# Twelve weight tiles of a hybrid decoder layer: low parts by an accumulating DMA in place of a VectorE subtract

## The chip, the core and the metric

The kernel runs on one core of a Trainium2 chip. The time is that of one execution on the device, in microseconds (us). Of several runs the median is given, with the lowest and the highest. Beside the runs, one execution was recorded by the profiler; its trace tells when each instruction ran on each engine. The engines are named as in the profile: PE (TensorE, matmuls), DVE (VectorE), ACT (ScalarE), POOL (GpSimd) and SP (SyncE, here only an issuer of DMAs).

## What is computed

One layer of a decoder trunk over 16 meta tokens and 1024 tokens of width 1024, in float32. Cut to what matters here:

```python
z = h @ w_in + b_in                       # 1024 -> 512 q, 128 k, 128 v, 2 x 512 conv, 2 x 1024 gates
a = swa_sink_attention(q, k, v, sinks, rel_bias)
c = c_val * jax.nn.sigmoid(c_gate)
c = jax.nn.silu(layer_norm(causal_dwconv(c, conv_dw, conv_dw_b), conv_ln_g, conv_ln_b))   # 31 taps
mixed = sigmoid(g_attn) * (a @ w_attn_proj) + sigmoid(g_conv) * (c @ w_conv_proj)
h = layer_norm(ALPHA * h + mixed @ w_out, ln1_g, ln1_b)
f = (gelu(g) * u) @ ffn_w_down            # u, g = split(causal_dwconv(h @ ffn_w_up)), 3 taps
h = layer_norm(ALPHA * h + f, ln2_g, ln2_b)
```

## The kernel before

**Precision by split operands.** Every float32 operand of a matmul is held as two float32r tiles: a high part (the value rounded to float32r) and a low part (value minus high part). A product is three matmuls, low x high, high x high, high x low, into the same PSUM bank (`product`, L336 to L345). So each weight tile passes through a split before TensorE may use it: `split` (L299 to L303) lets ScalarE copy the raw float32 tile into the high part (L300) and VectorE subtract the high part from the raw tile into the low part (L303).

**Weight tiles.** `weights` (L318 to L334) delivers a tile of 128 x 1024 (all 1024 rows of the weight, 128 output columns, as eight blocks of 128 columns). It takes a raw buffer from the pool `wraw` (tag `wr`, two buffers), has SP load it (`fill`), takes a pair of high and low parts from the pool `wsp` (tag `w`, two buffers) and splits. It counts its calls; below, tile n is the n-th call. Tiles 1 to 30 are those of `w_z`, the in-projection (L357 to L359: a tile's output for four groups of some 260 columns, 96 matmuls and 11 us on TensorE where nothing else stands between). Tiles 1 to 14 are k, v, q, most of the conv input and gates 0 and 1; tiles 15 to 17 gates 2 to 4, tiles 18 and 19 the last conv chunk, tiles 20 to 30 gates 5 to 15. Tiles 31 to 38 are those of `w_ab` (the loop over m at L1162), whose 128 output columns of the attention projection and of the conv projection are formed together and merged with the gates; there a product takes high x high, high x low, low x high (L1157 to L1172), so that the low part of the weight is read by the third matmul.

With two buffers of `w`, the copy of tile n waits until TensorE has read the last of tile n-2, which is the moment at which it begins tile n-1; so each tile is split while TensorE works on the tile ahead. With two buffers of `wr`, SP loads the raw tile n+2 as soon as the split of tile n has read its own.

**What stands beside.** From 171 to about 326 us TensorE alternates tiles 15 to 24 with banded attention (scores L919 and L920, transposes L943), while VectorE runs the depthwise conv, 31 taps for each of four chunks (L747, L749), GpSimd adds the chunks up once the third is done (`csum`, L972 and L973) and the rest of the LayerNorm over the conv follows up to about 385 us (mean by ones matmuls L982 and L984, squares L1030 and L1033, variance, roots L1045, silu L1057, splits L1063 and L1064). Gate outputs leave PSUM by a ScalarE tanh (L758) and are stored to a scratch `sgd` in DRAM by a DMA that ScalarE issues (L129). From 412 to about 500 us follow the eight tiles of `w_ab`. Per tile and group VectorE multiplies the gates by the two PSUM results (L1183, L1184), adds (L1185), and ScalarE and VectorE split the result (L1192, L1193). The gates come back from `sgd` by SP, four loads to a tile, into five slots of `OB`. The matmul results of the first branch lie in three PSUM buffers of tag `mm`, which the in-projection uses too, those of the second in two of tag `t`.

**What sets the order.** The program is written against a scheduler that simulates the engines and orders the instructions of each engine by rank (`with rank(...)`) and readiness. A split has rank 500, an evacuation 600, which come ahead of nearly all else that is ready. The order of each engine is thus fixed when the program is built, and each engine runs its list in order.

## Time and profile before

| | us |
|---|---|
| median of 3 runs | 1255.88 (1255.16 to 1256.59) |
| span of the profiled execution | 1253.2 |
| TensorE busy in it | 1239.1 |
| VectorE busy | 1078.1 |
| ScalarE busy | 627.4 |
| GpSimd busy | 7.4 |

For the profiled execution the span is the time that is known; the runs' median is 2.7 us longer. Busy time leaves out the issuing of DMAs and waits. A row of a timeline gives start, duration, engine, line, operation, out<-in, shape, and in brackets the idle time ahead of it with what ended it. A row of the waits gives the waiting engine and line, what it waited for, and the total, the number and the longest in us. The mean granted clock of TensorE was 0.999 of its full rate.

### The profile page before, as it was taken

What the parts mean: (1) busy time and instruction counts of PE and PEld (TensorE: products, weight loads), DVE (VectorE), ACT (ScalarE), POOL (GpSimd) and SP (SyncE); (2) the same over time, 40 slices, a digit from 0 to 9 for tenths busy, and PEclk for the clock granted to TensorE, in tenths of its full rate; (3) what the DMA queues carried; (4) which work ended last, traced back from release to release, by engine and by line L of the source; (5) the groups of instructions that cost most, each with busy time, mean ns of one, the idle gap of its engine ahead of it and who ended that gap; (6) DMA issues with size and microseconds to landing.
All of it is one profiled execution on the core that took longest, in us unless ns stands there. A gap on an engine that the chain in (4) does not pass through costs nothing.

```text
span 1253.2 us, 23194 instructions
## 1 busy us (share of the span) xinstructions
PE 1239.1 (99%) x9176; PEld 1173.8 (94%) x9176; DVE 1078.1 (86%) x1862; ACT 627.4 (50%) x1284; POOL 7.4 (1%) x8
## 2 busy tenths in 40 slices
PE   8999999999999999999999999999999999999997
PEld 7999999999999999788899999999999998888886
DVE  8989999999978677448899999998999977896697
ACT  8533255655474233344676556565565654545330
POOL 0000000001000000000000000000000000000000
PEclk9999999999999999999999999999999999999999
DMA  7383633432256564222145555453454567998712
GB/s 261 117 292 102 191 93 98 109 95 81 73 157 173 170 164 119 85 94 75 68 160 191 194 197 201 161 211 137 163 206 175 196 227 251 395 342 330 276 60 84
DMA packets 98687, 212.20 MB, mean 169 GB/s; under 512 B 11395, under 2 KB 38595, under 8 KB 98322
## 3 DMA queue, kind: packets, MB, share of 16 engines
q1 hardware_dynamic: 84414, 199.57, 46.9%
q10 hardware_dynamic: 14164, 11.15, 2.8%
q8 instruction: 72, 1.18, 0.4%
q14 instruction: 37, 0.30, 0.1%
HBM read 150.29 MB, written 62.70 MB: 170 GB/s over the span
## 4 chain that ended last, share of the span: by engine, by line
PE 96%; DVE 2%; ACT 1%; DMA 1%; issue 0%; SPq 0%; DVEq 0%; ACTq 0%
PE px L1594 15%; PE py L1594 10%; PE ps_x L1739 9%; PE ps_z L340 8%; PE ps_z L343 8%; PE ps_z L344 8%; PE ps_z L1739 7%; PE ps_p L1172 7%; PE pz L1594 5%; PE pw L1594 5%; PE ps_w L344 2%; PE ps_w L343 2%; PE ps_w L340 2%; PE ps_z L575 2%; PE ps_t L943 1%; PE ps_s L919 1%
## 5 line engine op out<-in xcount | busy, mean ns | idle before, releaser
L340 PE MATMUL ps_z<-RHO,w 128*128 128x256 f32 (+2 forms) x864 | 243.2, 281 | 0.0
L343 PE MATMUL ps_z<-RHO,w 128*128 128x256 f32 (+2 forms) x864 | 242.3, 280 | 0.0
L344 PE MATMUL ps_z<-RHC,w 128*128 128x256 f32 (+2 forms) x864 | 242.2, 280 | 0.0
L343 PEld LDWEIGHTS ps_z<-RHO,w 128*128 128x128 f32 x864 | 162.5, 188 | 0.5
L344 PEld LDWEIGHTS ps_z<-RHC,w 128*128 128x128 f32 x864 | 162.7, 188 | 0.2
L340 PEld LDWEIGHTS ps_z<-RHO,w 128*128 128x128 f32 x864 | 162.5, 188 | 0.1
L749 DVE SCALAR_TENSOR_TENSOR FA<-cin,cdw,FA 128x1026 f32<-128x1026 f32 x120 | 154.3, 1295 | 0.7
L300 ACT CAST w<-wr 128x1024 fp32r<-128x1024 f32 x37 | 38.8, 1048 | 64.0 <-PE ps_z L344 48.0
L1412 DVE TENSOR_TENSOR RHO<-wr,RHO 128x512 fp32r<-128x512 f32 x94 | 64.0, 684 | 3.6 <-ACT RHO L1411 3.5
L1411 ACT CAST RHO<-wr 128x512 fp32r<-128x512 f32 x94 | 56.9, 619 | 15.6 <-DVE wr L1429 7.9
L1429 DVE TENSOR_TENSOR wr<-wr 128x512 f32<-128x512 f32 x88 | 60.1, 683 | 0.1
L758 ACT ACTIVATE FA<-ps_z,colr 128x258 f32<-128x258 f32 (+1 forms) x64 | 30.1, 472 | 59.0 <-PE ps_z L344 50.7
L303 DVE TENSOR_TENSOR w<-wr,w 128x1024 fp32r<-128x1024 f32 x37 | 45.1, 1218 | 7.6 <-ACT w L300 7.4
L1606 ACT COPY FA<-px 128x516 f32<-128x516 f32 (+2 forms) x23 | 13.1, 571 | 71.2 <-PE px L1594 71.2
L1172 PE MATMUL ps_p<-OC,w 128*128 128x256 f32 (+1 forms) x384 | 48.1, 278 | 0.0
L1172 PE MATMUL ps_p<-OA,w 128*128 128x256 f32 (+1 forms) x384 | 47.8, 278 | 0.0
L1172 PEld LDWEIGHTS ps_p<-OC,w 128*128 128x128 f32 x384 | 46.2, 188 | 0.1
L1172 PEld LDWEIGHTS ps_p<-OA,w 128*128 128x128 f32 x384 | 45.9, 188 | 0.0
L1412 DVE TENSOR_TENSOR w<-wr,w 128x512 fp32r<-128x512 f32 x60 | 40.7, 684 | 4.7 <-ACT w L1411 4.7
L1594 PE MATMUL px<-OA,RHO 128*128 128x260 f32 x324 | 43.0, 282 | 0.0
L1594 PE MATMUL px<-OC,RHO 128*128 128x256 f32 x324 | 41.2, 276 | 0.8 <-DVE OB L1345 0.8
L1594 PE MATMUL px<-RHC,RHO 128*128 128x256 f32 (+1 forms) x312 | 40.6, 279 | 0.1
(457 smaller groups left out, 3109.3 us busy)
## 6 DMA issues: line engine op xcount, KB each, us to landing
wr<-in_w_up_dram SPq DMA_DIRECT2D x44, 512.0 KB, 3.6
wr<-in_w_z_dram SPq DMA_DIRECT2D x29, 512.0 KB, 4.2
OB<-in_w_down_dram SPq DMA_DIRECT2D x24, 512.0 KB, 5.2
fd<-FA SPq DMA_DIRECT2D x44, 256.0 KB, 2.0
FA<-sd SPq DMA_DIRECT2D x15, 512.0 KB, 8.9
qt<-qd SPq DMA_DIRECT2D x28, 256.0 KB, 4.1
OB<-td SPq DMA_DIRECT2D x14, 512.0 KB, 8.7
sgd<-FA ACTq DMA_DIRECT2D x48, 128.0 KB, 2.4
```

The costliest lines, as they stand in the source:

```text
L300: ins = nc.scalar.copy(hi, raw)
L303: return nc.vector.tensor_tensor(lo, raw, f32(hi), OP.subtract)
L340: ins = nc.tensor.matmul(ps, al, bh, start=i == 0, stop=False)
L343: nc.tensor.matmul(ps, ah, bh, start=False, stop=False)
L344: last = nc.tensor.matmul(ps, ah, bl, start=False, stop=i == n - 1)
L749: nc.vector.scalar_tensor_tensor(acc[c], cin[:, j:j + U], wc, acc[c], OP.mult, OP.add)
L1172: nc.tensor.matmul(ps[:, :b - a], x, rhs(k, hl, a, b), start=k + j == 0, stop=k == 3 and j == 2)
L1411: nc.scalar.copy(hi, src)
L1412: ins = nc.vector.tensor_tensor(lo, src, f32(hi), OP.subtract)
L1429: ins = nc.vector.tensor_tensor(*x)
L1594: ins = nc.tensor.matmul(o, (ah, ah, al)[j][:, k * P:(k + 1) * P], bmat(sub, q, j, k), start=first and i == 0, stop=i == 11, skip_group_ch ...
L1739: nc.tensor.matmul(banks[i], l[:, ts], r[:, ws], start=first and a and x + k == 0, stop=z and x == len(ops) - 1 and k == 2, skip_group_che ...
```

## The change

Odd tiles above 14, twelve in all (15, 17, 19, 21, 23, 25, 27 and 29 of the in-projection, 31, 33, 35 and 37 of `w_ab`), get their low part in another way. ScalarE copies the high part as before and then writes the negative of the high part into the low part's place. Two DMAs issued by GpSimd, one for the partitions 0 to 63 and one for 64 to 127, then add the raw tile to what stands there. VectorE's subtract of these tiles is gone. The raw buffer comes free when the DMAs have landed. [...]

```diff
-    colr = constr.tile([P, n_right], F, name="colr")
+    colr = constr.tile([P, n_right + 8], F, name="colr")[:, :n_right]
...
         hi, lo = chunks(sp.tile([P, W_LEN], R, name="w3") if own else wsp())
         if n <= 3:
             return hi, lo, raw
+        if n > 14 and n % 2:
+            with rank(RK_SPLIT):
+                nc.scalar.copy(hi, raw)
+                nc.scalar.mul(lo, f32(hi), -1.0)
+                for p in (0, 64):
+                    nc.gpsimd.dma_start(out=f32(lo)[p:p + 64], in_=raw[p:p + 64], accum_op=OP.add)
+            return hi, lo
         with rank(RK_SPLIT):
             last_split.append(split(raw, hi, lo))
...
-    OC = late.tile([P, 8376], R, name="OC")
+    OC = late.tile([P, 8320], R, name="OC")
...
-    nc = _bacc.Bacc("TRN2", target_bir_lowering=False, num_devices=1, dynamic_dma_scratch_size=64)
+    nc = _bacc.Bacc("TRN2", target_bir_lowering=False, num_devices=1, dynamic_dma_scratch_size=256)
```

The lines behind the new branch stand 7 further on in the changed kernel (L758 is L765 there, L1192 is L1199). The copy of a changed tile is L330, the multiplication L331, the DMAs L333.

ScalarE's list at the copy of tile 35, which is made while tile 34 is on TensorE (`RHO`, `RHC` and `pair` are splits of the merged result, `RX` a split of an output weight). Before:

```order
L1192 ACTIVATE RHO<-OB 128x2x128
L300 CAST w<-wr 128x1024
L1192 ACTIVATE RHC<-OB 128x2x128
L300 CAST RX<-FA 128x1024
L1187 ACTIVATE pair<-OB 128x2
```

The same place after:

```order
L1199 ACTIVATE RHO<-OB 128x2x128
L330 CAST w<-wr 128x1024
L1199 ACTIVATE RHC<-OB 128x2x128
L300 CAST RX<-FA 128x1024
L331 ACTIVATE w<-w 128x1024
L1194 ACTIVATE pair<-OB 128x2
```

The multiplication stands two instructions behind its copy, with another full-sized CAST between; in most of the twelve places it is one short instruction.

SP's list at the raw tiles 37 and 38 and the first of two output weights that use the same buffers (`wr<-in_w_ab_dram` is a raw tile, `OB<-sgd` the gates of one group, 258 columns for the first group of a tile). Before:

```order
L125 DMA FA<-in_w_out_dram 128x1024
L125 DMA wr<-in_w_ab_dram 128x1024
L125 DMA OB<-sgd 128x2x258
L125 DMA OB<-sgd 128x2x256 x3
L125 DMA wr<-in_w_ab_dram 128x1024
L125 DMA OB<-sgd 128x2x258
L125 DMA OB<-sgd 128x2x256 x3
L125 DMA wr<-in_w_out_dram 128x1024
L125 DMA OB<-sgd 128x2x258
L125 DMA OB<-sgd 128x2x256 x3
```

The same place after:

```order
L125 DMA FA<-in_w_out_dram 128x1024
L125 DMA OB<-sgd 128x2x258
L125 DMA OB<-sgd 128x2x256
L125 DMA wr<-in_w_ab_dram 128x1024
L125 DMA OB<-sgd 128x2x256 x2
L125 DMA wr<-in_w_ab_dram 128x1024
L125 DMA OB<-sgd 128x2x258
L125 DMA OB<-sgd 128x2x256 x3
L125 DMA OB<-sgd 128x2x258
L125 DMA wr<-in_w_out_dram 128x1024
L125 DMA OB<-sgd 128x2x256 x3
```

The load that waits for the DMAs of tile 35 now stands between the gate loads of a tile, two ahead of it and two behind; the one that waits for those of tile 37 has one gate load ahead and three behind.

On GpSimd the eight DMAs of tiles 15, 17, 19 and 21 stand ahead of the two additions for `csum`, the sixteen others behind them. TensorE's list is the same up to about 170 us and from the first `w_ab` tile on; between, attention's matmuls stand somewhat earlier among those of the tiles, and the mean's matmuls of the LayerNorm stand 18 matmuls earlier. VectorE's list loses the 12 subtracts and is otherwise reordered in the attention stage.

## Prediction

> **What bounds the kernel now.** I read first the busy times of the page, then the chain that ended last, then the waits of TensorE, then the three stretches in which the twelve changed tiles are prepared.

> From the page of the profile, the busy times and the chain by engine:

> ```profile
> PE 1239.1 (99%) x9176; PEld 1173.8 (94%) x9176; DVE 1078.1 (86%) x1862; ACT 627.4 (50%) x1284; POOL 7.4 (1%) x8
> PE 96%; DVE 2%; ACT 1%; DMA 1%; issue 0%; SPq 0%; DVEq 0%; ACTq 0%
> ```

> From the view of waits, TensorE's own (in total, times, longest, in us):

> ```profile
> PE ps_w L590 <- DVE ones L239: 1.7, 1, 1.7
> PE ps_h L518 <- DVE xn L497: 1.5, 1, 1.5
> PE pw L1594 <- ACT FA L1392: 1.2, 1, 1.2
> PE px L1594 <- DVE OB L1345: 0.8, 1, 0.8
> PE ps_z L572 <- ACT FA L524: 0.3, 1, 0.3
> PE ps_s L919 <- DVE sm L923: 0.3, 1, 0.3
> ```

> From the view of windows, the in-projection tiles beside conv and attention, the last of them beside the conv LayerNorm, and the two-branch projection:

> ```profile
> core 0: us, PE busy (x) PEld busy (x) DVE busy (x) ACT busy (x) POOL busy (x), PEclk, DMA share, GB/s
> 171.00:326.00 155.00, 154.69 (x1259) 151.40 (x1257) 151.36 (x324) 85.49 (x227) 5.30 (x2) 1.00 0.34 95
> 326.00:413.00 87.00, 87.00 (x740) 86.50 (x739) 72.64 (x133) 46.34 (x79) 0.00 (x0) 1.00 0.54 152
> 413.00:480.00 67.00, 67.00 (x583) 67.00 (x582) 47.38 (x110) 18.77 (x40) 0.00 (x0) 1.00 0.54 151
> ```

> The reader is to see that TensorE does the chain by itself (96%), waits six times in the whole program, and in the three stretches is busy for 154.69 + 87.00 + 67.00 = 308.69 of 309.00 us at a granted clock of 1.00. VectorE is busy for 151.36 of 155 us in the first stretch, close behind, but TensorE waits for it there once, for 0.3 us. So in the changed stretch a shorter queue on VectorE can give back at most 0.3 us, as long as a matmul takes the time that it takes now.

> **The change, part by part.** The split of a tile has two rows in the page's costliest groups:

> ```profile
> L300 ACT CAST w<-wr 128x1024 fp32r<-128x1024 f32 x37 | 38.8, 1048 | 64.0 <-PE ps_z L344 48.0
> L303 DVE TENSOR_TENSOR w<-wr,w 128x1024 fp32r<-128x1024 f32 x37 | 45.1, 1218 | 7.6 <-ACT w L300 7.4
> ```

> Removed: 12 subtracts of 1.218 us = 14.6 us of VectorE. It has no row in TensorE's waits but the 0.3 us, so this is worth 0 to 0.3 us; I take 0.

> Added on ScalarE: 12 multiplications of a 128x1024 tile. The row nearest is the CAST of the same shape on the same engine, so 12 x 1.05 = 12.6 us. ScalarE is busy for 85.49 of 155, 46.34 of 87 and 18.77 of 67 us: it has room. What is queued behind a multiplication are evacuations of PSUM, each later by up to 1.05 us; three buffers of the tag `mm` cover that except where ScalarE is full, between 356 and 385 us (a rival, below). I take 0.

> Added on GpSimd: 24 DMAs of 256 KB, two to a tile. GpSimd has two instructions in these stretches. Eight of the DMAs (tiles 15 to 21) stand ahead of them and sixteen behind, and those sixteen thus wait as well for what the first of the two waits for, the third chunk's taps. In the timeline these two, and the copies of tiles 23 to 26 on ScalarE:

> ```profile
> 282.13 2.43 POOL L972 TENSOR_TENSOR csum<-FA 128x1026 f32<-128x1026 f32 x1 [279.46 <-DVE FA L749]
> 284.63 2.87 POOL L973 TENSOR_TENSOR csum<-csum,FA 128x1026 f32<-128x1026 f32 x1
> ```

> ```profile
> 300.61 1.03 ACT L300 CAST w<-wr 128x1024 fp32r<-128x1024 f32 x1
> 316.48 1.05 ACT L300 CAST w<-wr 128x1024 fp32r<-128x1024 f32 x1 [1.12 <-PE ps_z L344]
> 331.10 1.05 ACT L300 CAST w<-wr 128x1024 fp32r<-128x1024 f32 x1 [1.94 <-PE ps_z L344]
> 343.66 1.05 ACT L300 CAST w<-wr 128x1024 fp32r<-128x1024 f32 x1 [2.24 <-PE ps_z L344]
> ```

> csum ends at 287.5, and tile 23, the first behind it, is copied at 300.61: 13 us to spare, so 0.

> Now the term that decides: **the new path of a low part**. Before, copy and subtract follow each other. Now copy, one ScalarE instruction of other work in most tiles, multiplication, then the two DMAs, and TensorE wants the low part in the first matmul of a z tile and in the third of a projection tile. The copy can't start sooner than the w buffer comes free, at the start of the tile ahead. In the view of the timeline, ScalarE and TensorE around tile 37 (the starts of tiles 35 and 37) and tile 35:

> ```profile
> 445.51 1.05 ACT L300 CAST w<-wr 128x1024 fp32r<-128x1024 f32 x1 [1.32 <-PE ps_p L1172]
> 446.46 0.41 ACT L1192 ACTIVATE RHC<-OB 128x256 fp32r<-128x256 f32 x1
> 446.78 1.03 ACT L300 CAST RX<-FA 128x1024 fp32r<-128x1024 f32 x1
> 456.33 0.28 PE L1172 MATMUL ps_p<-OA,w 128*128 128x258 f32 x1
> 467.64 1.05 ACT L300 CAST w<-wr 128x1024 fp32r<-128x1024 f32 x1 [0.98 <-PE ps_p L1172]
> 468.59 0.41 ACT L1192 ACTIVATE RHC<-OB 128x256 fp32r<-128x256 f32 x1
> 478.46 0.28 PE L1172 MATMUL ps_p<-OA,w 128*128 128x258 f32 x1
> ```

> Two tiles take 478.46 - 456.33 = 22.13 us, one 11.07. Tile 37: copy at 467.64, other work to 469.0, multiplication to about 470.05; TensorE comes at 478.46. That leaves the DMAs 8.4 us. Tiles 27, 31 and 33 have the same pattern (copy at the start of the tile ahead, one to three short instructions, multiplication), so I take 8.4 for each. Tile 35 has the CAST into RX ahead of its multiplication as well: 446.78 + 1.03 + 1.05 = 448.86, which leaves 456.33 - 448.86 = 7.5. Tile 29 is the tight one, since ScalarE reaches its copy late:

> ```profile
> 382.94 1.04 ACT L300 CAST w<-wr 128x1024 fp32r<-128x1024 f32 x1
> 383.88 0.83 ACT L758 ACTIVATE FA<-ps_z,colr 128x256 f32<-128x256 f32 x2
> 389.97 0.28 PE L340 MATMUL ps_z<-RHO,w 128*128 128x258 f32 x1
> ```

> Copy to 383.98, one evacuation to 384.4, multiplication to 385.4: 4.6 us are left. In the changed order ScalarE's LayerNorm work begins some 2 us earlier (the matmuls of the mean stand 18 matmuls earlier on TensorE, 2.1 us at the second stretch's 87.00 / 740 = 0.118 us each), so up to 6.6; I take the middle, 5.6. Tiles 15 to 25 have more, because attention's matmuls stand in the tiles ahead of them: from copy to copy it is 331.10 to 343.66 = 12.6 us at tile 25 and 15.9 at tile 23, so 9.9 us are left at tile 25 and over that before.

> Against these stands **T, from the end of the multiplication to the landing of both halves**. No row of this trace shows a DMA from GpSimd or one that accumulates. The nearest rows (KB each, median us from issue to landing):

> ```profile
> qt<-qd SPq DMA_DIRECT2D x28, 256.0 KB, 4.1
> wr<-in_w_z_dram SPq DMA_DIRECT2D x29, 512.0 KB, 4.2
> sd<-sums SPq DMA_DIRECT2D x12, 512.0 KB, 2.6
> raw<-fd SPq DMA_DIRECT2D x5, 512.0 KB, 9.8
> OB<-sgd SPq DMA_DIRECT2D x21, 256.0 KB, 3.4
> ```

> qt is the nearest: the same 64 partitions of 4 KB. Two of them at once give 4.1, one after the other 8.2. The ends are 2.6 (512 KB out of SBUF in one) and 9.8 (the slowest row of that size). I take 6.2, the middle of 4.1 and 8.2, as the two halves may overlap in part. Then only tile 29 is late, by 6.2 - 5.6 = 0.6 us. At 2.6 or 4.1 nothing is late. At 8.2 tile 29 loses 2.6 (1.6 to 3.6) and tile 35 0.7: 3.3. At 9.8 tile 29 loses 4.2, tile 35 2.3 and tiles 27, 31, 33 and 37 1.4 each, 5.6: 12.1. [...]

> **The queue of SP.** The raw tile two further on may be loaded when the low part is done, before after the subtract (1.05 + 1.22 = 2.3 us after the copy's start), now after the landing, some 2.4 + 6.2 = 8.6 us after it. It takes 4.2 us and is wanted 22.1 us after the copy's start, so the weight itself is early by 22.1 - 12.8 = 9.3 us. What is queued behind it on SP are the gate loads (sgd): a rival.

> **Sum.** On the profiled execution: span 1253.2 us, +0.6 = 1253.8. The median of the runs, 1255.88, is 2.7 over the span; with the same 2.7 I predict 1256.5. About 0.2% of the time, 2.5 us, is what a measurement of this kernel can tell from no change.

> **The rivals.**

> A, my forecast: the low parts are in time but for tile 29. 1256.5, and between -0.3 and +1.6 us, 1255.6 to 1257.5, with what the runs scatter (0.7) 1254.9 to 1258.2. For it: 8.4 us of room in most tiles against 4.1 in the nearest row.

> B, slower: T is over 8 us, and TensorE waits at the head of the short tiles. It decides from about T = 8.0. +3.3 at 8.2 (1259.2), +12.1 at 9.8 (1268.0). For it: an accumulating DMA reads twice, two halves behind each other are twice the nearest row, and 9.8 stands in the trace. Against: other 512 KB rows show 2.6 and 4.2. [...] I give that mechanism 0.08 and B in all 0.23.

> C, slower by queues: a raw load that waits on SP for a landing holds the gate loads behind it. In the timeline SP's four gate loads of a tile, VectorE's use of the second of them, and a table load of ScalarE in the LayerNorm stage:

> ```profile
> 470.64 7.80 SPq L125 DMA_DIRECT2D OB<-sgd  x4
> 481.60 0.41 DVE L1183 SCALAR_TENSOR_TENSOR OB<-OB,ps_p 128x256 f32<-128x256 f32 x1
> 362.25 1.28 ACT L1045 ACT_TABLE_LOAD   x1
> ```

> In the changed order the load behind tile 37's DMAs stands ahead of three of those four loads. They would be issued at 470.05 + T; with 3.4 us to land, the first is late from T = 481.60 - 470.05 - 3.4 = 8.1 on, and two PSUM buffers of tag `t` stand between that and TensorE. The other place of this kind is ScalarE between 356 and 385 us, where a multiplication (1.05) and one more table load (1.28) stand against a start 2.1 us earlier: +0.2, or +2.3 if the earlier start doesn't come. At T = 8.8 the gate loads are 0.7 late behind tile 35's DMAs and behind tile 37's, 1.4; with the 2.3 that makes +3.7, 1259.6; chance 0.07.

> D, faster by over 2.5 us: only if matmuls are issued closer when VectorE and attention press less, for which the windows leave 0.3 us of waiting. Were 1% of the first stretch's 155 us so gained and the same in the next, 2.4 us: 1253.5. Chance 0.06.

> That the change does not do what it says is no rival here: the changed order holds all 24 DMAs and none of the 12 subtracts.

> **How the numbers follow.** A 0.64, B 0.23, C 0.07, D 0.06. B and C are slower by over 0.2% in nearly all their cases; the mild end of each stays under it, as the slow edge of A goes over it, and I let these cancel: slower 0.30, same 0.64, faster 0.06. The range takes in A whole (1254.9 to 1258.2), D's nearer half (to 1254.2) and B up to about T = 8.4 with C, 1261.0; outside are D's rest (0.03) and B's far part (0.14).

> **What would show it.** Right: no wait of TensorE for `w` in the view of waits but one of about 0.6 us at tile 29; twelve rows of 1.05 us on ScalarE; the DMAs of GpSimd at 6.2 us for a pair; VectorE's busy time lower by 14.6 us with an unchanged span. Wrong: a wait of TensorE for a DMA of `w` at the heads of several tiles (B), idle time of VectorE at L1190 for a gate load or TensorE waiting for a PSUM buffer (C), or a shorter stretch from 171 to 413 us (D).

## The result, and the profile after

The changed kernel takes 1278.41 us (median of 4 runs, 1275.40 to 1279.08) against 1255.52 us (4 runs) for the kernel before on the same chip. The ratio is 1.0183, with a 95% interval of 1.0171 to 1.0195: 23 us slower, where 1256.5 was forecast and 1261.0 was the upper end of the range.

In the profiled execution the span grew from 1253.2 to 1276.1 us, by 22.9. Busy times and chain of the page:

```profile
PE 1247.0 (98%) x9176; PEld 1180.3 (92%) x9176; DVE 1064.0 (83%) x1850; ACT 639.6 (50%) x1297; POOL 27.4 (2%) x32
PE 91%; DMA 3%; DVE 2%; issue 2%; ACT 1%; POOL 0%; SPq 0%; DVEq 0%; ACTq 0%
```

VectorE lost 14.1 us and ScalarE gained 12.2, as costed (14.6 and 12.6). But TensorE's share of the chain fell from 96% to 91%, and that of DMA rose from 1% to 3%. TensorE's waits in the changed kernel (in total, times, longest):

```profile
PE ps_z L347 <- DMA w<-wr: 7.9, 3, 4.2
PE ps_p L1179 <- DMA w<-wr: 4.5, 2, 2.5
PE ps_h L525 <- DVE xn L504: 2.0, 1, 2.0
PE ps_w L597 <- DVE ones L239: 1.7, 1, 1.7
PE ps_p L1179 <- ACT RHC L1199: 1.2, 1, 1.2
PE pw L1601 <- ACT FA L1399: 1.2, 1, 1.2
PE ps_p L1179 <- ACT w L300: 1.0, 1, 1.0
```

New are seven waits of 14.6 us: five for a DMA of `w` (7.9 + 4.5) and two put down to ScalarE (1.2 + 1.0), which are the same thing, as the rows of tile 37 show. ScalarE, GpSimd and TensorE in the timeline there:

```profile
489.98 0.41 ACT L1199 ACTIVATE RHC<-OB 128x256 fp32r<-128x256 f32 x1
490.29 1.04 ACT L331 ACTIVATE w<-w 128x1024 fp32r<-128x1024 f32 x1
491.74 0.82 POOL L333 DMA_DIRECT2D w<-wr  x1 [17.66 <-ACT w L331]
496.82 0.82 POOL L333 DMA_DIRECT2D w<-wr  x1 [4.26 <-issue]
499.84 0.40 PE L1179 MATMUL ps_p<-OA,w 128*128 128x258 f32 x2
501.45 0.73 PE L1179 MATMUL ps_p<-OA,w 128*128 128x258 f32 x4 [1.20 <-ACT RHC L1199]
```

TensorE does its first two matmuls, which need only the high part, at 499.84 and stands until 501.45. The ScalarE instruction named as releaser (L1199) was done at 490.39, long before; what came at 501.3 was the second DMA, issued at 496.82. The rows also tell why it came so late: the second half was issued 5.08 us after the first, with 4.26 us ahead of it in which GpSimd waited for nothing that the profile shows ("issue"). From issue to landing a half takes (view of the line L333):

```profile
DMA to landing us min/median/max: 4.5/4.9/5.5
```

So T, from the end of the multiplication at 491.33 to the landing of both, is 0.4 + 5.1 + 4.5 = 10.0 us at tile 37. Over the twelve tiles it is 9.8 to 11.6, with a median of 10.4. Tile 37 had 8.5 us of room.

The same three stretches as before, and then the 4 us behind three of the waits (the first of each pair) beside 4 us a little later, all for the changed kernel:

```profile
171.00:326.00 155.00, 155.00 (x1254) 151.21 (x1253) 151.98 (x332) 91.57 (x240) 13.65 (x12) 1.00 0.49 108
326.00:413.00 87.00, 79.12 (x643) 78.41 (x642) 63.38 (x124) 46.04 (x76) 5.07 (x6) 0.96 0.65 152
413.00:480.00 67.00, 61.58 (x509) 61.04 (x508) 30.84 (x73) 19.85 (x36) 4.93 (x6) 0.97 0.64 151
346.60:350.60 4.00, 4.00 (x21) 4.00 (x22) 0.37 (x1) 0.00 (x0) 0.00 (x0) 0.57 0.84 189
350.60:354.60 4.00, 4.00 (x35) 4.00 (x34) 2.75 (x8) 2.44 (x6) 0.00 (x0) 1.00 1.06 301
401.00:405.00 4.00, 4.00 (x22) 4.00 (x23) 3.79 (x10) 0.00 (x0) 0.00 (x0) 0.58 0.67 174
405.00:409.00 4.00, 4.00 (x36) 4.00 (x36) 3.83 (x9) 0.96 (x2) 0.00 (x0) 0.99 0.97 309
428.00:432.00 4.00, 3.92 (x21) 3.95 (x22) 0.42 (x1) 0.00 (x0) 0.00 (x0) 0.62 0.67 232
436.00:440.00 4.00, 4.00 (x37) 4.00 (x36) 2.46 (x8) 0.84 (x2) 0.00 (x0) 1.00 0.02 4
```

The first stretch is as busy as before. In the other two TensorE stands idle, and the granted clock is no longer 1.00. Behind three of the seven waits it is 0.57 to 0.62 for 4 us, and 14, 14 and 16 matmuls fewer are done there than in the 4 us compared: at 0.114, 0.111 and 0.108 us each, 1.6 + 1.6 + 1.7 = 4.9 us. TensorE counts as busy meanwhile, so most of the growth of its busy time (7.9 us) is this.

Waits 14.6 and slow clock 4.9 make 19.5 of 22.9 us. Of the other 3.4, 1.3 are not the change's own: they are lost in the first 30 us of the program, long before the first changed tile, where from 12.5 to 15.9 us the clock is at 0.50 in this execution and at 1.00 in that of before. And 1.1 are the waits' again: the view counts a wait from the end of the matmul ahead; counted from start to start, less the 0.11 us between two matmuls, the seven are 15.7 us. Some 1 us stays without an explanation.

### The profile page after: what moved, and what is told of

Its sections match the earlier page's. It is cut to its first block, busy times and chain, and to the rows that moved or that the text cites. A ratio compares the mean times of both kernels' runs of the same rounds, so it can differ in the third digit from the quotient of the medians.

```text
span 1276.1 us, 23267 instructions
## 1 busy us (share of the span) xinstructions
PE 1247.0 (98%) x9176; PEld 1180.3 (92%) x9176; DVE 1064.0 (83%) x1850; ACT 639.6 (50%) x1297; POOL 27.4 (2%) x32
## 4 chain that ended last, share of the span: by engine, by line
PE 91%; DMA 3%; DVE 2%; issue 2%; ACT 1%; POOL 0%; SPq 0%; DVEq 0%; ACTq 0%
PE px L1601 14%; PE py L1601 10%; PE ps_x L1746 9%; PE ps_z L1746 7%; PE ps_z L347 7%; PE ps_z L350 7%; PE ps_z L351 7%; PE ps_p L1179 5%; PE pw L1601 5%; PE pz L1601 5%; PE ps_w L351 2%; PE ps_w L347 2%; PE ps_w L350 2%; PE ps_z L582 2%; DMA w<-wr 2%
## 5 line engine op out<-in xcount | busy, mean ns | idle before, releaser
L765 ACT ACTIVATE FA<-ps_z,colr 128x258 f32<-128x258 f32 (+1 forms) x64 | 30.3, 473 | 62.0 <-PE ps_z L351 56.6
L1179 PE MATMUL ps_p<-OA,w 128*128 128x256 f32 (+1 forms) x384 | 50.6, 285 | 6.6 <-DMA w<-wr 4.5
L300 ACT CAST w<-wr 128x1024 fp32r<-128x1024 f32 x25 | 26.2, 1047 | 47.5 <-PE ps_z L351 37.4
L303 DVE TENSOR_TENSOR w<-wr,w 128x1024 fp32r<-128x1024 f32 x25 | 30.5, 1218 | 22.9 <-ACT w L300 22.8
L1601 PEld LDWEIGHTS px<-OA,RHO 128*128 128x128 f32 x324 | 40.4, 188 | 0.2 <-ACT OB L1613 0.2
## 6 DMA issues: line engine op xcount, KB each, us to landing
wr<-in_w_up_dram SPq DMA_DIRECT2D x44, 512.0 KB, 4.3
wr<-in_w_z_dram SPq DMA_DIRECT2D x29, 512.0 KB, 3.8
OB<-in_w_down_dram SPq DMA_DIRECT2D x24, 512.0 KB, 4.8
fd<-FA SPq DMA_DIRECT2D x44, 256.0 KB, 2.0
FA<-sd SPq DMA_DIRECT2D x15, 512.0 KB, 9.1
qt<-qd SPq DMA_DIRECT2D x28, 256.0 KB, 5.0
OB<-td SPq DMA_DIRECT2D x14, 512.0 KB, 8.7
```

Of the source, the lines that this page charges most:

```text
L303: return nc.vector.tensor_tensor(lo, raw, f32(hi), OP.subtract)
L765: nc.scalar.activation(t, ps, AF.Tanh, bias=bcol(14 + i), scale=0.5)
L1179: nc.tensor.matmul(ps[:, :b - a], x, rhs(k, hl, a, b), start=k + j == 0, stop=k == 3 and j == 2)
L1601: ins = nc.tensor.matmul(o, (ah, ah, al)[j][:, k * P:(k + 1) * P], bmat(sub, q, j, k), start=first and i == 0, stop=i == 11, skip_group_ch ...
```

## The experiments

Each run is compared with runs of the kernel before on the same chip, whose median was 1254.77 us (vector_add, room_320, plain_copy, quarters), 1254.28 (shift_only, room_same_place, covered_tiles, room_skip_29_35), 1255.24 (vector_add_skip_27, whole_same_place) and 1255.31 (whole_skip_27, halves_skip_29).

### vector_add: the landing taken away

```diff
-                for p in (0, 64):
-                    nc.gpsimd.dma_start(out=f32(lo)[p:p + 64], in_=raw[p:p + 64], accum_op=OP.add)
+                nc.vector.tensor_tensor(lo, raw, f32(lo), OP.add)
```

> The changed kernel with a VectorE addition (raw plus negative high part) in place of the two DMAs; the multiplication on ScalarE, the sizes and the scratch stay. Theory (all of the loss is the late landing and what follows from it): 1255 to 1257. Rival (ScalarE's added multiplication, the changed order of attention and LayerNorm, or the shifted layout cost part): above 1257, up to 1260 for the 2 us that the trace does not put down to waits for the DMAs and the slow matmuls after them.

Measured 1257.73 us, ratio 1.0026 (1.0016 to 1.0036). So without the DMAs 20 us of the 23 are gone; 3 us stay, and for them the rival holds. TensorE's order is not that of the changed kernel here (in 1004 of 9176 places another matmul stands), so this run alone doesn't prove that the 20 us are the DMAs'; `plain_copy` below, which keeps every order, gives the same 20. The trace has no wait for `w`, and one new wait, in the LayerNorm stage:

```profile
PE ps_z L346 <- ACT FA L764: 0.8, 1, 0.8
```

The changed kernel has no such wait; around the same stage it has those for a DMA of `w`, from 344 and from 372 us.

### vector_add_skip_27: what the 3 us are

```diff
-        if n > 14 and n % 2:
+        if n > 14 and n % 2 and n != 27:
```

> vector_add without tile 27, whose split is then the old one. Theory: what vector_add is slower by (2 to 3 us) is mostly one stall of TensorE at 375 us, where the multiplication of tile 27 and one more pair of table loads made ScalarE evacuate PSUM late; without it ScalarE is 1 us ahead there, the stall of 1.1 us is gone or below 0.5, and the time is 1255 to 1256.5. Rival (the changed order itself, with its extra table loads, makes the stall): still over 0.5 us of stall there and 1256.5 to 1258.

Measured 1255.11 us, 0.9998 (0.9989 to 1.0007), with no stall of TensorE in the changed stretch. Without tile 27's multiplication ScalarE's list also has two table loads for evacuations (L764) in the LayerNorm stage again, as before the change, in place of three. The multiplication and the table loads went together in this run, so it does not tell their shares.

### room_320: can the second half follow at once?

```diff
-    nc = _bacc.Bacc("TRN2", target_bir_lowering=False, num_devices=1, dynamic_dma_scratch_size=256)
+    nc = _bacc.Bacc("TRN2", target_bir_lowering=False, num_devices=1, dynamic_dma_scratch_size=320)
```

> The changed kernel with a descriptor scratch of 320 in place of 256, and nothing else. Theory (room): the second half of each pair was issued 0.3 us after the first had landed because the scratch holds the descriptors of only one half. Then here the second is issued about 1 us after the first, both have landed some 0.4 + 1 + 5 = 6.5 us after the multiplication in place of 10.4, no tile but perhaps tile 29 is late, and the time is 1256 to 1259. Rival (one at a time): GpSimd starts no DMA before its last one has landed, whatever the room; then issues stay some 5.2 us apart and the time stays at 1277 to 1279. Rival (transfer): the halves are issued close together but share what moves them, the second lands as late as now, and the time is 1272 or more.

Measured 1275.12 us, 1.0162 (1.0147 to 1.0177). The issue did what the theory said, the time did not. GpSimd in its trace issues both halves of tile 37 in one go, 0.54 us apart where it was 5.1:

```profile
478.18 1.67 POOL L333 DMA_DIRECT2D w<-wr  x2 [20.07 <-ACT w L331]
```

and the waits put down to a DMA of `w` are down from 12.4 to 3.5 us:

```profile
PE ps_z L347 <- DMA w<-wr: 3.5, 2, 3.1
```

But some 12 us of the gain are lost elsewhere, to the end of the program. The groups of TensorE that read `OC` show where (columns: busy, mean ns of one), in room_320:

```profile
L1601 PE MATMUL px<-OC,RHO 128*128 128x256 f32 x324 | 43.0, 282 | 0.8 <-DVE OB L1352 0.8
L1601 PE MATMUL px<-OC,w 128*128 128x256 f32 x204 | 27.0, 282 | 0.0
```

and in the kernel before:

```profile
L1594 PE MATMUL px<-OC,RHO 128*128 128x256 f32 x324 | 41.2, 276 | 0.8 <-DVE OB L1345 0.8
L1594 PE MATMUL px<-OC,w 128*128 128x256 f32 x204 | 25.9, 276 | 0.0
```

Each takes 6 ns more. The program has `w`, `RHO` and `OA` in pools of the side "left" and `OC` in one of the side "right". My reading, an estimate from the sizes in the program, is that 64 more of scratch push the tiles on the left up by 64 bytes, while `OC` stays; no trace shows where a tile lies. In the change itself, `OC` is 56 columns shorter and `colr` 8 longer, 192 bytes together, as much as the scratch grew (256 - 64), so that by this reading both sides moved alike and kept their distance. Two runs test this.

### shift_only: the displacement by itself

```diff
-    nc = _bacc.Bacc("TRN2", target_bir_lowering=False, num_devices=1, dynamic_dma_scratch_size=64)
+    nc = _bacc.Bacc("TRN2", target_bir_lowering=False, num_devices=1, dynamic_dma_scratch_size=128)
```

> The kernel before with a scratch of 128 in place of 64 and nothing else: no DMA from GpSimd, only 64 bytes of displacement of the tiles on the left side against those on the right. Theory of the displacement: +10 to +14 us, 1265 to 1269, with OC's matmuls at 119 ns. Rival: no difference, 1255.

Measured 1266.98 us, 1.0101 (1.0086 to 1.0116): 12.7 us for 64 more of scratch, with the program's work and every engine's order unchanged. Its row for the same group:

```profile
L1594 PE MATMUL px<-OC,RHO 128*128 128x256 f32 x324 | 43.0, 282 | 0.8 <-DVE OB L1345 0.8
```

All groups that read `OC` together are busy 10.3 us longer, which is most of it. Why is not shown: the group `py<-RHC,RHO` grows as well (276 to 281 ns), though both of its tiles are in one pool on the left.

### room_same_place: both halves at once, nothing displaced

```diff
-    coll = const.tile([P, n_kept - n_right + 24], F, name="coll")[:, :n_kept - n_right]
+    coll = const.tile([P, n_kept - n_right + 8], F, name="coll")[:, :n_kept - n_right]
```

(with the scratch of 320)

> Scratch 320 as before this, but 16 spare columns of the tile coll are taken out, so that every other tile lies where it lies in the changed kernel; the order of every engine is the same. Theory: of the 20 us that room_320 lost, some 12 came from 64 bytes of displacement between the tiles on the two sides of the scratch (its matmuls on OC took 119 ns instead of 113 to the end of the program), and the rest from T = 7.4 to 9 us at tiles 25 and 29 and from ScalarE in the LayerNorm stage. Then here 1260 to 1263, OC's matmuls at 113 ns, and T as in room_320. Rival: the 12 us belong to the larger scratch or to the overlapping DMAs; then 1273 or more.

Measured 1263.73 us, 1.0071 (1.0056 to 1.0086), 0.7 us above what was expected. The displacement is out (the group `px<-OC,RHO` is at 276 ns again), and 64 more of scratch make the changed kernel 1.0183 - 1.0071 = 1.12% faster, 14 us. In this run nothing else differs from the changed kernel but where `coll` ends; every engine's order is the same. The first halves land 4.5 to 5.6 us after their issue, much as alone, the second 6.4 to 8.1:

```profile
DMA to landing us min/median/max: 4.5/6.0/8.0
```

The second landed 7.3 to 9.0 us after the multiplication, and tile 29, whose room is the smallest, kept a wait of 3.0 us.

### plain_copy: without the accumulation

```diff
-                    nc.gpsimd.dma_start(out=f32(lo)[p:p + 64], in_=raw[p:p + 64], accum_op=OP.add)
+                    nc.gpsimd.dma_start(out=f32(lo)[p:p + 64], in_=raw[p:p + 64])
```

> The changed kernel with the accumulation left out of the 24 DMAs: they copy the raw weights over the negative high part, so the addition is not done and the low parts hold other numbers. The scratch stays at 256. Room: a DMA that does not read its target needs fewer descriptors, so two halves fit; the second is issued about 1 us after the first, and the time is 1255 to 1259. One at a time: issues still 4 to 5 us apart, 1270 or more. The landing of one half against 4.9 us tells what the accumulation itself costs.

Measured 1256.79 us, 1.0021 (1.0009 to 1.0033). With the scratch of 256 both are issued together here:

```profile
471.18 1.06 POOL L333 DMA_DIRECT2D w<-wr  x2 [20.12 <-ACT w L331]
```

```profile
DMA to landing us min/median/max: 2.8/4.1/8.0
```

The pair lands 4.6 to 6.8 us after the multiplication in eleven of twelve tiles (9.0 at tile 31). So it was the accumulating form of the DMA that did not fit twice, and the accumulation costs 6.0 - 4.1 = 1.9 us in the median of a half beside another, 2.2 to 3.4 us in the pair at ten of twelve tiles (room_same_place against this run; 0.5 and 0.0 at tiles 19 and 31). Nine of the twelve copies keep within the 6.2 us of the prediction.

### quarters: four DMAs to a tile

```diff
-                for p in (0, 64):
-                    nc.gpsimd.dma_start(out=f32(lo)[p:p + 64], in_=raw[p:p + 64], accum_op=OP.add)
+                for p in (0, 32, 64, 96):
+                    nc.gpsimd.dma_start(out=f32(lo)[p:p + 32], in_=raw[p:p + 32], accum_op=OP.add)
```

> The changed kernel with four DMAs of 32 partitions to a tile in place of two of 64; scratch 256. Room: a quarter needs about half the descriptors of a half, so two or three quarters are in flight and the last waits for the first; all landed 8 to 11 us after the multiplication, 1268 to 1282. One at a time: four landings in a row, at least 4 x 3.5 = 14 us after the multiplication, so at least 4 us more at each of eight tiles, over 1305.

Measured 1265.18 us (two runs), 1.0082 (1.0057 to 1.0106), 3 us below the range that the theory of room gave and far from one at a time. For tile 37 three are issued together, and the fourth 1.63 us after them:

```profile
479.19 2.36 POOL L333 DMA_DIRECT2D w<-wr  x3 [17.73 <-ACT w L331]
483.19 0.77 POOL L333 DMA_DIRECT2D w<-wr  x1 [1.63 <-issue]
```

The first lands 3.69 us after its issue at 479.19 and the fourth follows 0.31 us later, at the same distance at which the second half followed the landing of the first in the changed kernel (0.3 at all twelve tiles). All four have landed after 7.5 to 8.7 us at ten of twelve tiles, and after 9.5 and 11.1 at tiles 29 and 31.

### whole_same_place: one DMA to a tile

```diff
-                for p in (0, 64):
-                    nc.gpsimd.dma_start(out=f32(lo)[p:p + 64], in_=raw[p:p + 64], accum_op=OP.add)
+                nc.gpsimd.dma_start(out=f32(lo), in_=raw, accum_op=OP.add)
```

(on room_same_place)

> room_same_place with one DMA of 128 partitions in place of two of 64. If what is left of T is the work of the transfer (reading two tiles and writing one, 512 KB, beside the other traffic), the one DMA lands as late as the second half did, 7.4 to 9 us after the multiplication, and the time is 1260 to 1264. If the second issue and the fixed part of a DMA count, it lands a us or more sooner, 6 to 7.5, and the time is 1257 to 1260.

Measured 1258.50 us, 1.0026 (1.0015 to 1.0036). One DMA of 512 KB lands as soon as one half did:

```profile
w<-wr POOLq DMA_DIRECT2D x12, 512.0 KB, 5.0
```

It has landed 5.0 to 7.3 us after the multiplication at eleven tiles, at most of them sooner than either reading expected, and 8.6 us after it at tile 31. TensorE waits for no DMA of `w`; its waits in the changed stretch are for ScalarE's LayerNorm work and, once, for the attention.

### whole_skip_27: both remedies

Tile 27 left out as above, on whole_same_place.

> whole_same_place without tile 27: eleven tiles by one accumulating DMA each, tile 27 by the old split. Theory: with the landing inside the room of every tile but by chance tile 31 (8.6 us against 8.5), and ScalarE's LayerNorm stage as before (two table loads for evacuations in place of three), nothing is left that TensorE waits for: 1254.5 to 1256.5, no gain from the 13 us less on VectorE. Rival (the DMAs or multiplications cost by themselves): 1257 or more.

Measured 1257.22 us, 1.0020 (1.0012 to 1.0029), above what the theory gave and in the range of the rival. Again no wait for a DMA, but the LayerNorm stage still has one for an evacuation:

```profile
PE ps_z L346 <- ACT FA L764: 1.5, 1, 1.5
```

so that leaving out tile 27 does not remove it in this order, as it did in vector_add_skip_27. This wait is most of the 1.9 us; which instruction of ScalarE makes it no run tells, and so whether the multiplications cost by themselves stays open. None of the variants beats the kernel before.

### covered_tiles: only the tiles with long tiles ahead

```diff
-        if n > 14 and n % 2:
+        if 14 < n < 24 and n % 2:
```

> The change for tiles 15, 17, 19, 21 and 23 alone; the seven others keep VectorE's subtract. Theory: 10.4 us of landing are hidden behind tiles of 14 us and more, so the time is that of before but for the changed order of attention, 1255 to 1257, and no wait for a DMA of w. Rival: the multiplications, the DMA traffic or the raw loads that wait for landings cost something by themselves in the crowded stretch: 1258 or more.

Measured 1255.66 us, 1.0009 (1.0000 to 1.0019). The halves come 4.9 to 5.3 us apart there too, and land 9.8 to 10.7 us after the multiplication, but the five tiles have 11 to 15 us: a late landing that is covered costs 0.1%, which the interval hardly tells from nothing.

### room_skip_29_35 and halves_skip_29: do the stalls add up?

Tiles 29 and 35 left out on room_same_place, and tile 29 on the changed kernel.

> Scratch 320 with every tile in its place, and tiles 29 and 35 keep VectorE's subtract. Theory: with T at 7.4 to 9 us and 8.5 us of room at the other tiles, what is left are fractions of a us at single tiles and ScalarE's LayerNorm stage: 1256 to 1259. Rival (the stalls only move to the next changed tile): 1261 or more.

Measured 1261.97 us, 1.0064 (1.0040 to 1.0088): not the theory's number but the rival's, 1261 or more. The wait at tile 29 went, and another came at tile 31, with 3.4 us of granted clock at 0.50 behind it:

```profile
PE ps_p L1179 <- DMA w<-wr: 2.2, 1, 2.2
```

> The changed kernel (scratch 256, halves) without tile 29. Theory: its stall of 4.5 us goes, and on average the slow clock behind it (1.6 us where it came), the other stalls stay: 1271 to 1274. Rival (the stalls are passed on, a tile that is no longer late leaves the next one later): 1276 or more.

Measured 1272.94 us, 1.0139 (1.0126 to 1.0152), the number expected, but not by that sum alone: tile 31's wait grew here too, to the longest of all:

```profile
PE ps_p L1179 <- DMA w<-wr: 8.8, 2, 6.9
```

In both the first half of tile 31 took 8.5 and 9.5 us to land, where other tiles have 5. With tile 29 on time, tile 31's DMAs are issued earlier, and in every variant in which that was so they were slow (a plain copy 6.2 us, the one whole DMA 8.2). SP loads the first gates and an output weight about there; whether those hold it up no run shows.

## Why the prediction was wrong

**What bounds the kernel** was read rightly. VectorE's 14 us are worth nothing: whole_skip_27, with eleven subtracts gone and no wait for a DMA, and covered_tiles, with five gone, are no faster than the kernel before.

**The step that failed is T.** "I take 6.2, the middle of 4.1 and 8.2, as the two halves may overlap in part." They don't overlap at all: the second is issued 0.3 us after the first has landed, and T is 10.4 in the median, over the upper end of 9.8. The runs show two parts in it. The order of the halves: with 64 more of scratch they are issued 0.54 us apart and T is 7.3 to 9.0 (room_same_place, 14 us faster). The accumulation: a plain copy has 4.6 to 6.8 at eleven of twelve tiles. The rows that I took for T were single loads or copies from another queue, and the diff said by the scratch that this queue has room to run out of: a sign that the prediction does not weigh. What fills the scratch, descriptors or other, and how much of it a half takes no run shows; how many go out together does: at 256 three quarters, two copies or one accumulating half, at 320 two halves.

**The room** held where the order of TensorE was unchanged: 8.5 us at tile 37 and 7.6 at tile 35 (predicted 8.4 and 7.5). At tile 29 it was 6.5, inside 4.6 to 6.6. At tile 25 it was 8.5 and not 9.9: with attention's matmuls placed earlier, tile 24 has none left, so tile 25 was late as well, and I had read its room from the old order. With T = 10.4, 6.5 at one tile, 7.6 at one and 8.5 at the five others give 3.9 + 2.8 + 5 x 1.9 = 16.2 us against 14.6 of waits. So rival B was the case, with T at 10.4 and seven tiles late.

**What the sum did not have** is the price of a wait beyond its length, the 4.9 us of slow clock. The prediction has it only as a condition, "as long as a matmul takes the time that it takes now". In the changed kernel's trace the clock behind three waits is at 0.50 for 3.41 us each time, and these stretches begin at 347.03, 401.64 and 428.95 us, 54.61 and 27.31 us apart, 16 and 8 times 3.41. Divided into windows of this length, counted from those starts, the trace shows the windows ahead of two slow ones, and one behind which the clock stays (columns: length, busy time of TensorE, PEclk, DMA share, GB/s):

```profile
343.62:347.03 3.41, 1.45 (x12) 1.00 0.76 100
347.03:350.44 3.41, 3.41 (x18) 0.50 0.93 197
370.92:374.33 3.41, 1.73 (x15) 1.00 0.75 101
374.33:377.74 3.41, 3.41 (x31) 1.00 0.56 156
398.22:401.63 3.41, 0.76 (x6) 1.00 0.57 79
401.64:405.05 3.41, 3.41 (x18) 0.50 0.79 206
```

In quarters a wait of 3.4 us falls half into one window and half into the next and has no slow clock behind it, while a wait of 1.9 us, which lies within one window, has:

```profile
PE ps_z L347 <- DMA w<-wr: 3.4, 1, 3.4
```

```profile
388.68:392.09 3.41, 1.75 (x15) 1.00 0.95 197
392.09:395.50 3.41, 1.65 (x14) 1.00 0.36 92
395.51:398.92 3.41, 3.41 (x32) 1.00 0.99 321
415.99:419.40 3.41, 1.54 (x14) 1.00 0.69 210
419.40:422.81 3.41, 3.41 (x19) 0.50 0.70 231
```

So it is in all five traces with a slow stretch behind a wait (the changed kernel, quarters, room_320, room_skip_29_35, halves_skip_29): the nine windows in which TensorE was busy for 1.54 us or less are followed by one at half clock, and no window with 1.65 us or more is. In these traces a wait of about 2 us thus cost another 1.7 us (half of 3.41) or nothing, by where in a window it fell: that part of the price is chance.

**VectorE as a part of T** (0.08 of B) is not shown: a first half landed in 4.6 to 5.0 us in the first stretch, where VectorE is busy for 151.98 of 155 us, and in 4.5 to 4.8 at tiles 33, 35 and 37, while VectorE was busy for 2.93 of 4.70, 3.15 of 4.70 and 3.06 of 4.80 us. The medians, 4.9 and 4.6, leave 0.3 us for it. So no run shows the T = 8.8 that stands in the sum of rival C; the runs showed a T of 9.8 to 11.6, two landings in a row.

**The queues** (rival C): SP's gate loads never made TensorE wait. ScalarE's LayerNorm stage did in the variants whose DMAs are in time, by 0.7 us of wait (plain_copy) to 2.4 (whole_same_place), out of the 2 to 3 us that remain there; the two ends given were +0.2 and +2.3. I had it with a chance of 0.07 and kept it out of the sum.

## What to carry to other kernels

Work taken off an engine that nothing waited for gave nothing here (14.1 us of VectorE), and its replacement had to be measured by its latency (10.4 us) against the room of the tightest tile (6.5), not by the busy time that it frees. Before several DMAs are given to one queue, see in a timeline whether the second is issued before the first lands (5.1 us after the first with a scratch of 256, 0.54 with 320); here one whole DMA landed as soon as one of the two halves (5.0 and 4.9 us). Where sizes change for the layout's sake, compare the mean of the same matmul group before and after (276 and 282 ns here).
